# Three column blocks of the second modulation multiplied and added up on GpSimd in a hybrid S5 and attention block on one Trainium2 core

## Chip, core and metric

The kernel runs on one core of one Trainium2 chip. The metric is the device time of one execution in microseconds (us). Everything here is one launch; weights, input and output lie in the chip's memory outside the core.

## The reference, cut to what is computed

One decoder layer over 256 tokens of width 2048:

```python
mod = silu(c) @ w_ada + b_ada
shift1, scale1, gate1, shift2, scale2, gate2 = split(mod, 6)
h = rms(x, norm1_w) * (1 + scale1) + shift1
u, q, k, v = split(h @ w_in)
y_ssm = s5_mixer(u)
y_att = dilated_attention(q, k, v)
x = x + gate1 * (concat([y_ssm, y_att]) @ w_out)
h2 = rms(x, norm2_w) * (1 + scale2) + shift2
x = x + gate2 * ((silu(h2 @ w_ffn_gate) * (h2 @ w_ffn_up)) @ w_ffn_down)
```

`mod` is a product of one row, `silu(c)`, with a matrix of 2048 x 12288: nearly all of its cost is to read the matrix. The second modulation is `shift2` and `scale2`, each 2048 columns, cut into four blocks of 512 columns: eight blocks. They are needed only when `h2` is made, after the output projection.

## The kernel before

All big products run in pairs of rounded halves: ScalarE copies a loaded weight tile into `whi` (L135), VectorE makes the rest `wlo` (L137), and TensorE multiplies three times (`mm_tok`, L154). Each weight tile is 128 x 1024 floats, 512 KB. SyncE's queue issues all of them in an order fixed by the program (`load`, L110), into a **ring of six buffers** named `raw`. Load n+6 goes into the buffer of load n, so it is issued only when all who read load n are done, and every later load stands behind it in that queue.

The stages in order: the first modulation together with the products for `u` and the first `q` block; then five blocks of q, k and v columns, eight weight tiles each, so 40 steps of twelve matmuls over 512 columns (tile `qkv`); eight steps for the gate of the S5 part (tile `z`); 32 steps of the output projection (`wo`, `wol`); then the feed-forward part (`ff`, `dn`).

After each weight tile's matmuls, `step()` lets side work advance. Side work is made of Python generators: `lanes` (S5 batches `ssm_batch` with products S and y, attention heads `head`, query and key posts), and the modulation stream `ada_stream`, which is advanced 1.6 times per step in the first 30 steps and 0.9 times after. One advance of the stream stands for about one load of `w_ada`. A cost that a generator hands back is taken from the budget of 2.2 that the lanes get in a step.

In `ada_stream` a load of `w_ada` goes through TensorE: a column of `silu(c)` against the tile (L255, tile `ada`). A block of 512 columns is eight loads. After a set of blocks the sums are copied out and turned into columns by a small matmul, `ada_finish` (L212, tile `adac`). `DV` names blocks that do not go this way: `ada_dve` takes them, one block here (scale2's last). VectorE multiplies each half tile by a column of `silu(c)` and adds it to `gv` in one instruction (L310, L312), sixteen per block, and `ada_finish` turns `gv` with four matmuls against ones. `ada_next` would mix this generator in from its 80th call on; the stream drains it before that, at its own end (L271). After that the stream waits until seven of eight S5 batches are done and then goes through `gate1`, 32 loads on VectorE (L292).

GpSimd clears tiles (L512 to L589, L277) and issues the DMAs that reorder the S5 output: `yd` to memory (L780), then four `yT` back (L783), for each of eight batches.

Which instruction stands where on SyncE is the program's order. On the other engines a scheduler sets it when the program is built, from priorities in program order and its own estimate of when operands are ready. An engine runs its list in order and stops at a wait.

Of the kernel before, what the change touches and what calls it, by code (L numbers as in the profile page):

```python
# [11 lines left out]
ALU = mybir.AluOpType  # L12
# [26 lines left out]
NEX = 1.6  # L39
NEX2 = 0.9  # L40
NDB = 7
DV = ((4, 12, 4),)
DV0 = 80
DVS = 6
GPE = ()
QN_ACT = True
NS1 = 30
# [14 lines left out]
def body(tc, sm, tabs, bc, brow, x, wada, wg2, win, wglu, wout, wgate, wup, wdown, out):  # L62
    nc = tc.nc
    V, A, PE, G, SP = nc.vector, nc.scalar, nc.tensor, nc.gpsimd, nc.sync
# [43 lines left out]
    def load(src):  # L108
        raw = ring.tile([128, 2, 512], F32, name="raw", bufs=RAW)
        SP.dma_start(raw.rearrange("p k n -> p (k n)"), src)  # L110
        return raw
# [95 lines left out]
    def ada_finish(parts, ev, whole=False):  # L207
        kind, g0, ng = parts[0]
        n = len(parts)
        pc = ms([128, ng, n], "adac")  # L210
        for j in range(ng):
            PE.matmul(pc[:, j], lhsT=ev[:, j * 128:(j + 1) * 128], rhs=ones[:, 0:1] if whole else sel[:, 0:n], start=True, stop=True)  # L212
        for i, (kind, g0, _) in enumerate(parts):
            cols = slice(g0, g0 + ng)
            n, bn, wn = MOD[kind]
            V.tensor_tensor(out=gcol[n][:, cols], in0=pc[:, :, i], in1=col(bn)[:, cols], op=ALU.add)
            if wn:
                V.scalar_tensor_tensor(out=gcol[n][:, cols], in0=gcol[n][:, cols], scalar=1.0, in1=col(wn)[:, cols],
                                       op0=ALU.add, op1=ALU.mult)
        if kind < 2:  # L220
            h_hook[0](g0 // 2)

    def ada_stream(sets):
# [45 lines left out]
            yield  # L269
        ada_finish(*pend)  # L270
        for _ in adv:  # L271
            yield 1.2
        while len(done_b) < NDB:
            yield
        g = P8([128, D], "gate1")
# [5 lines left out]
        for b in range(4):  # L281
            gb = g[:, b * 512:(b + 1) * 512]
            ps = ada_ps
            for h in range(8):
                wt = load(wada[8 + b, h])
# [15 lines left out]
    def ada_dve():  # L301

        for kind, g0, ng in DV:
            gv = p1.tile([128, 512], F32, name="gv", tag="gv", bufs=1)
            for h in range(8):
                wt = load(wada[kind * 4 + g0 // 4, h])
                for j in range(2):
                    c = cs[:, 2 * h + j:2 * h + j + 1]
                    if h + j == 0:
                        ts(gv, wt[:, j], c, None, ALU.mult)  # L310
                    else:
                        V.scalar_tensor_tensor(out=gv, in0=wt[:, j], scalar=c, in1=gv, op0=ALU.mult, op1=ALU.add)  # L312
                yield 1.2
            yield
            ada_finish([(kind, g0, ng)], gv, True)

    ada = ada_stream([[(0, 2 * p, 2), (1, 2 * p, 2)] for p in range(8)]
                     + [[v for v in [(k, 4 * b, 4) for b in range(4)] if v not in DV] for k in (3, 4)])
    adv = ada_dve()
    adn = [0]  # L320

    def ada_next():
        adn[0] += 1
        if adn[0] >= DV0 and adn[0] % DVS == 0:
            c = next(adv, -1.0)
            if c != -1.0:
                return c or 0.0
        return next(ada, None) or 0.0


# [38 lines left out]
    def ts(o, a, s1_, s2_, o0, o1=None):  # L369
        if o1 is None:  # L370
            V.tensor_scalar(out=o, in0=a, scalar1=s1_, scalar2=None, op0=o0)
        else:
            V.tensor_scalar(out=o, in0=a, scalar1=s1_, scalar2=s2_, op0=o0, op1=o1)
# [511 lines left out]
    nstep = [0]  # L885

    def one(ln):

        while ln:
            try:  # L890
                return next(ln[0])
            except StopIteration:
                ln.pop(0)
        return None
# [6 lines left out]
    def step(budget=SB):  # L901
        nstep[0] += 1
        debt[0] = max(debt[0] - budget, -budget)
        pace = lambda n: int(min(n, NS1) * NEX + max(n - NS1, 0) * NEX2)
        for _ in range(pace(nstep[0]) - pace(nstep[0] - 1)):
            debt[0] += ada_next()
        turn[0] ^= 1
        live = [{0: turn[0], 1: 1 - turn[0], 2: 2, 3: 3}[i] for i in LORD] * LM
        stop = set()
        for k in live:  # L910
            if debt[0] < 0 and k not in stop:
                c_ = one(lanes[k])
                if c_ is None:
                    stop.add(k)
                else:
                    debt[0] += c_
# [8 lines left out]
    for b in range(2):  # L925
        for which, blk in ((0, 2 + b), (1, 4 + b), (2, 6 + b)):
            if blk == 2:
                lanes[3].append(qk_post(b, which, q0))
                continue
            ps = acc([128, 2, 512], "qkv")  # L930
            for hf in range(8):
                hl = take()
                for j in range(2):
                    kc = hf * 2 + j
                    mm_tok(ps, lambda a, t: hT[kc // 4][:, kc % 4, a, t * 128:(t + 1) * 128], hl, j, kc == 0, kc == 15)
                step()
            if which < 2:
                lanes[3].append(qk_post(b, which, ps))
            else:
                lanes[3].append(v_post(b, ps))  # L940
                for h in range(4):
                    lanes[2 + h % 2 * b].append(head(b, h))
# [3 lines left out]
    for nb in range(2):  # L946
        z = acc([128, 4, 256], "z")
        for hf in range(4):
            hl = take()
            for j in range(2):  # L950
                kc = hf * 2 + j
                for c in range(4):
                    w = slice(c * 128, c * 128 + 128)
                    for n, (wt, a) in enumerate(((hl[0], 0), (hl[0], 1), (hl[1], 0))):
                        PE.matmul(z[:, c], lhsT=wt[:, j, w], rhs=yT[kc // 4][:, kc % 4, a], start=(kc == 0 and n == 0 and c % 2 == 0),
                                  stop=(kc == 7 and n == 2), skip_group_check=True)
            step()
        th_ = T4([128, 4, 256], "zth")
        nat = lambda v: v.rearrange("p m (r j) -> p m j r", r=4)
        tq = lambda v: v.rearrange("p m (j r) -> p m j r", r=4)  # L960
        for c in range(4):
            A.activation(tq(th_)[:, c], nat(z)[:, c], AF.Tanh, scale=0.5)
        yy = T4([128, 4, 256], "zy")
        for c in range(4):
            tt(tq(yy)[:, c], nat(yT[nb][:, :, 0].bitcast(F32))[:, c], nat(yT[nb][:, :, 1].bitcast(F32))[:, c], ALU.add)
        V.scalar_tensor_tensor(out=yy, in0=th_, scalar=1.0, in1=yy, op0=ALU.add, op1=ALU.mult)
        mt = act.tile([128, 4, 2, 256], F32R, name="mixS", tag="act", bufs=4)
        A.mul(mt[:, :, 0], yy, 0.5)
        V.scalar_tensor_tensor(out=mt[:, :, 1], in0=yy, scalar=0.5, in1=mt[:, :, 0].bitcast(F32), op0=ALU.mult, op1=ALU.subtract)
        mix.append(mt)  # L970
# [307 lines left out]
```

## Time and profile before

| what | value |
|---|---|
| median of three runs | 1247.48 us (1246.68 to 1251.21) |
| the profiled execution, its own time | 1248.12 us |
| its span, first to last instruction | 1246.3 us |
| TensorE busy (matmul) in the span | 1193.3 us |
| VectorE busy | 793.3 us |
| GpSimd busy | 50.5 us |

The table's busy times are sums over the whole span; a stage has its own limit, so the rows below are taken by stretches. A busy TensorE is not TensorE at its peak: spacing between matmuls is read from the chain of waits. Waits are put down to whichever awaited event came last.

### The profile page before, as it was taken

The numbers are of one execution on the slowest core, as the hardware profiler recorded it, in microseconds if no ns is written. First come the engines' busy times: TensorE is split into PE (matmuls) and PEld (weight loads), VectorE is DVE, ScalarE is ACT, GpSimd is POOL, SyncE is SP. The second block draws the span as 40 slices with busy tenths as digits, with TensorE's granted clock in tenths as the row PEclk, the third lists the DMA queues.
The fourth block names the chain that finished last, engine by engine and source line by source line (L and its number), as shares of the span: only waits on it lengthen the run. The fifth ranks groups of instructions, "written<-read, shape, count | busy, mean of one in ns | idle before, by whom it ended". The sixth has DMA issues, their size and how long they took to land.

```text
span 1246.3 us, 17021 instructions
## 1 busy us (share of the span) xinstructions
PE 1193.3 (96%) x6312; PEld 954.0 (77%) x6312; DVE 793.3 (64%) x1402; ACT 572.2 (46%) x871; POOL 50.5 (4%) x90
## 2 busy tenths in 40 slices
PE   4789899999998999899999999999999999999998
PEld 2567667667797777688888888888888878888886
DVE  7964766477879998855665565565555444545544
ACT  3654574456455445644444444444444443434332
POOL 1110001121120000000000000000000000000000
PEclk9899999999999999899999999999999999999999
DMA  9889878897996899367777777777766656666662
GB/s 378 314 289 365 311 265 293 287 305 265 327 318 205 300 338 338 120 212 241 233 241 224 240 241 241 230 228 248 236 187 187 197 161 199 207 197 205 197 208 67
DMA packets 93906, 306.85 MB, mean 246 GB/s; under 512 B 18080, under 2 KB 20544, under 8 KB 93184
## 3 DMA queue, kind: packets, MB, share of 16 engines
q1 hardware_dynamic: 80784, 294.69, 70.7%
q0 software_dynamic: 11312, 6.70, 2.7%
q10 hardware_dynamic: 1728, 4.38, 0.9%
q8 instruction: 49, 0.80, 0.3%
q14 instruction: 33, 0.27, 0.1%
HBM read 301.54 MB, written 4.19 MB: 245 GB/s over the span
## 4 chain that ended last, share of the span: by engine, by line
PE 79%; DVE 10%; DMA 5%; ACT 3%; issue 2%; POOL 0%; DVEq 0%; ACTq 0%; POOLq 0%
PE ff L154 38%; PE dn L154 14%; PE qkv L154 8%; PE dnl L154 5%; PE ada L255 3%; DMA raw<-wada 3%; DVE wlo L137 2%; PE uacc L639 2%; PE wo L154 2%; DMA raw<-win 1%; PE y L763 1%; PE S L733 1%; DVE gate L292 1%; PE q L154 1%; DVE wkt L368 1%
## 5 line engine op out<-in xcount | busy, mean ns | idle before, releaser
L137 DVE TENSOR_TENSOR wlo<-raw,whi 128x1024 fp32r<-128x1024 f32 x365 | 446.6, 1224 | 334.5 <-ACT whi L135 333.8
L135 ACT CAST whi<-raw 128x1024 fp32r<-128x1024 f32 x365 | 384.8, 1056 | 499.3 <-PE ff L154 270.1
L154 PE MATMUL ff<-whi,h2T 128*128 128x512 f32 x1408 | 438.5, 391 | 0.7 <-DVE h2T L1074 0.5
L154 PEld LDWEIGHTS ff<-whi,h2T 128*128 128x128 f32 x1408 | 264.6, 188 | 56.6 <-ACT h2T L1073 1.0
L154 PE MATMUL ff<-wlo,h2T 128*128 128x512 f32 x704 | 274.5, 390 | 0.0
L154 PE MATMUL dn<-whi,aT 128*128 128x512 f32 x528 | 163.4, 390 | 0.0
L154 PEld LDWEIGHTS ff<-wlo,h2T 128*128 128x128 f32 x704 | 132.5, 188 | 26.9
L154 PEld LDWEIGHTS dn<-whi,aT 128*128 128x128 f32 x528 | 99.1, 188 | 21.0 <-ACT whi L135 0.2
L154 PE MATMUL qkv<-whi,hT 128*128 128x512 f32 x320 | 108.1, 405 | 0.3 <-ACT whi L135 0.2
L154 PE MATMUL dn<-wlo,aT 128*128 128x512 f32 x264 | 103.1, 391 | 0.0
L154 PEld LDWEIGHTS qkv<-whi,hT 128*128 128x128 f32 x320 | 60.6, 190 | 25.5 <-issue 6.4
L154 PE MATMUL qkv<-wlo,hT 128*128 128x512 f32 x160 | 64.1, 401 | 2.0 <-DVE wlo L137 2.0
L1132 DVE SCALAR_TENSOR_TENSOR gate<-raw,cs,gate 128x1024 f32<-128x1024 f32 x32 | 41.1, 1284 | 38.3 <-DMA raw<-wg 38.3
L639 PE MATMUL uacc<-hT,whi 128*128 128x256 f32 x256 | 51.7, 299 | 6.9 <-ACT whi L135 6.9
L154 PEld LDWEIGHTS dn<-wlo,aT 128*128 128x128 f32 x264 | 49.6, 188 | 10.8 <-issue 0.5
L154 PE MATMUL dnl<-whi,aT 128*128 128x512 f32 x176 | 54.4, 389 | 0.0
L292 DVE SCALAR_TENSOR_TENSOR gate<-raw,cs,gate 128x512 f32<-128x512 f32 x64 | 48.0, 754 | 7.6 <-DMA raw<-wada 7.2
L639 PEld LDWEIGHTS uacc<-hT,whi 128*128 128x128 f32 x256 | 42.0, 201 | 13.5 <-ACT whi L135 9.9
L255 PE MATMUL ada<-raw,c 128*4 128x256 f32 (+1 forms) x496 | 50.7, 492 | 0.0
L639 PE MATMUL uacc<-hT,wlo 128*128 128x256 f32 x128 | 38.7, 302 | 5.7 <-DVE wlo L137 5.7
L154 PEld LDWEIGHTS dnl<-whi,aT 128*128 128x128 f32 x176 | 33.0, 188 | 7.0 <-DVE o L368 0.2
L154 PEld LDWEIGHTS qkv<-wlo,hT 128*128 128x128 f32 x160 | 30.5, 191 | 8.9 <-DVE wlo L137 2.3
(318 smaller groups left out, 1257.1 us busy)
## 6 DMA issues: line engine op xcount, KB each, us to landing
raw<-wada SPq DMA_DIRECT2D x130, 512.0 KB, 5.3
raw<-wgate SPq DMA_DIRECT2D x88, 512.0 KB, 4.3
raw<-wup SPq DMA_DIRECT2D x88, 512.0 KB, 4.1
raw<-wdown SPq DMA_DIRECT2D x88, 512.0 KB, 3.7
raw<-win SPq DMA_DIRECT2D x64, 512.0 KB, 5.5
raw<-wout SPq DMA_DIRECT2D x32, 512.0 KB, 4.9
raw<-wg SPq DMA_DIRECT2D x32, 512.0 KB, 4.0
rawp<-wada SPq DMA_DIRECT2D x30, 512.0 KB, 7.2
```

The lines of the kernel that those rows point to most:

```text
L135: A.copy(hi, raw)
L137: V.tensor_tensor(out=lo, in0=raw, in1=hi.bitcast(F32), op=ALU.subtract)
L154: PE.matmul(ps[t] if type(ps) is list else ps[:, t], lhsT=lhs(a, t), rhs=w[:, j], start=first and n == 0, stop=last and n == 2)
L255: PE.matmul(ps[32 * q:32 * q + 4, 0:w], lhsT=c7[:, kc, 3 - i:7 - i], rhs=wts[t][:, j * w:(j + 1) * w], start=q not in seen, stop=n == len( ...
L292: V.scalar_tensor_tensor(out=gb, in0=wt[:, j], scalar=cs[:, 2 * h + j:2 * h + j + 1], in1=gb, op0=ALU.mult, op1=ALU.add)
L368: V.tensor_tensor(out=o, in0=a, in1=b, op=op)
L639: PE.matmul(uacc[b][:, c], lhsT=wt[:, j, w], rhs=h[:, j, a], start=(kc == 0 and n == 0 and c % 2 == 0), stop=(kc == 15 and n == 2), skip_g ...
L733: PE.matmul(S[:, e, Q], lhsT=wv[:, 0, Q, e].rearrange("p i c -> p (i c)"), rhs=U[:, m, Q], start=True, stop=True)
L763: PE.matmul(y[:, Q], lhsT=Vt[:, Q, e].rearrange("p r c -> p (r c)"), rhs=hp[:, e, Q], start=False, stop=e == 1, skip_group_check=True)
L1132: V.scalar_tensor_tensor(out=g, in0=wt, scalar=cs[:, k:k + 1], in1=g, op0=ALU.mult, op1=ALU.add)
```

## The change

`DV` now names three blocks of scale2: columns 512 to 1023, 1024 to 1535 and 1536 to 2047. The first two leave `ada_stream` and so TensorE; the third was VectorE's. `ada_dve` now puts all three on GpSimd. What was one instruction of VectorE per half tile is two of GpSimd: a multiplication by a column in place (`raw` into `raw`, after the first half tile) and an addition to `gv`. `gv` still has one buffer. The generator hands back no cost any more. `step()` advances it 0.7 times per step by itself, and `ada_stream` still drains what is left of it when its own blocks are done.

```diff
-DV = ((4, 12, 4),)
-DV0 = 80
-DVS = 6
+DV = ((4, 4, 4), (4, 8, 4), (4, 12, 4))
+NPL = 0.7
@@ ada_stream
         for _ in adv:
-            yield 1.2
+            yield
@@ ada_dve
                     if h + j == 0:
-                        ts(gv, wt[:, j], c, None, ALU.mult)
+                        G.tensor_scalar(out=gv, in0=wt[:, j], scalar1=c, scalar2=None, op0=ALU.mult)
                     else:
-                        V.scalar_tensor_tensor(out=gv, in0=wt[:, j], scalar=c, in1=gv, op0=ALU.mult, op1=ALU.add)
-                yield 1.2
+                        G.tensor_scalar(out=wt[:, j], in0=wt[:, j], scalar1=c, scalar2=None, op0=ALU.mult)
+                        G.tensor_tensor(out=gv, in0=wt[:, j], in1=gv, op=ALU.add)
+                yield
@@ ada_next
-        adn[0] += 1
-        if adn[0] >= DV0 and adn[0] % DVS == 0:
-            c = next(adv, -1.0)
-            if c != -1.0:
-                return c or 0.0
         return next(ada, None) or 0.0
@@ step
         for _ in range(pace(nstep[0]) - pace(nstep[0] - 1)):
             debt[0] += ada_next()
+        if int(nstep[0] * NPL) > int((nstep[0] - 1) * NPL):
+            next(adv, None)
```

The built programs show what moved, at three places. In the changed file line numbers are a little lower: L109 is the load, L153 the big matmul, L211 the matmul of `ada_finish`, L309 to L312 the GpSimd instructions, L775 and L778 the reordering DMAs.

SyncE's queue in the second half of the q, k, v steps, before (`win` is a weight tile of a step; `wada` is a load of the modulation, here two at a time for TensorE, and after the `x3` one at a time for VectorE's block):

```order
L110 DMA raw<-win 128x1024 x2
L110 DMA raw<-wada 128x1024 x2
L110 DMA raw<-win 128x1024
L110 DMA raw<-wada 128x1024 x2
L110 DMA raw<-win 128x1024
L110 DMA raw<-wada 128x1024 x2
L110 DMA raw<-win 128x1024
L110 DMA raw<-wada 128x1024 x2
L110 DMA raw<-win 128x1024 x3
L110 DMA raw<-wada 128x1024
L110 DMA raw<-win 128x1024
```

The same queue in the change, from the same place; the first row is in both programs the 163rd and 164th load, counted from zero over all loads of that queue:

```order
L109 DMA raw<-win 128x1024 x2
L109 DMA raw<-wada 128x1024 x3
L109 DMA raw<-win 128x1024
L109 DMA raw<-wada 128x1024
L109 DMA raw<-win 128x1024
L109 DMA raw<-wada 128x1024 x2
L109 DMA raw<-win 128x1024
L109 DMA raw<-wada 128x1024 x3
L109 DMA raw<-win 128x1024
L109 DMA raw<-wada 128x1024 x2
L109 DMA raw<-win 128x1024 x13
L109 DMA raw<-wada 128x1024
```

All eleven `wada` loads ahead of the `x13` are GpSimd's now, with four `win` between them; TensorE's own loads of the modulation have all passed. The last `wada` is `gate1`'s first.

GpSimd's list in the change, near the end of its third block (`gv` is the running sum; the brackets name the counters that an instruction waits on, `Pool_49` being GpSimd's own):

```order
L311 TENSOR_SCALAR raw<-raw,cs 128x512
L312 TENSOR_TENSOR gv<-raw,gv 128x512 [waits Pool_49]
L775 DMA yd<-wks 256x1x256 [waits DMASW5_49,DVE_49]
L312 TENSOR_TENSOR gv<-raw,gv 128x512 [waits Pool_49]
L311 TENSOR_SCALAR raw<-raw,cs 128x512 [waits DMAHW4_49]
L311 TENSOR_SCALAR raw<-raw,cs 128x512
L312 TENSOR_TENSOR gv<-raw,gv 128x512 [waits Pool_49]
L778 DMA yT_1982<-yd 32x8x64 [waits DMASW6_49,DMASW5_49]
L312 TENSOR_TENSOR gv<-raw,gv 128x512 [waits Pool_49]
L311 TENSOR_SCALAR raw<-raw,cs 128x512 [waits DMAHW7_49,DMAHW5_49]
```

Four instructions now stand there per load, each addition waits for GpSimd's own earlier work, and the reordering DMAs stand in between.

TensorE's list in the change, at the end of the second `gv` block (`adac` is the small matmul on `gv`; `qkv` of the next weight tile stands behind it):

```order
L153 MATMUL qkv<-wlo,hT 128x512
L153 MATMUL qkv<-whi,hT 128x512
L211 MATMUL adac<-ones,gv 128x1 [waits PE_49,Pool_49]
L211 MATMUL adac<-ones,gv 128x1 x3
L728 MATMUL S<-U,wv 128x64 [waits PE_49]
```

Such a wait of TensorE on GpSimd stands at three places now, one per block. The third stands right behind the twelve matmuls of the first of the thirteen `win` tiles. Before, the one `adac` on `gv` waited for VectorE and stood among the `z` matmuls.

## Rows read from the trace of the kernel before

**Rows 1.** Busy time by stretch: length, busy us (instructions) per engine, clock, DMA share, GB/s

```profile
171.00:230.00 59.00, 56.65 (x325) 40.64 (x326) 43.38 (x122) 31.77 (x91) 7.85 (x16) 0.97 0.84 281
230.00:290.00 60.00, 57.27 (x358) 39.31 (x356) 37.51 (x106) 29.45 (x58) 9.84 (x15) 1.00 0.89 279
290.00:355.00 65.00, 65.00 (x384) 50.71 (x384) 54.23 (x129) 34.38 (x86) 9.02 (x13) 1.00 0.93 311
355.00:402.00 47.00, 43.94 (x298) 39.97 (x298) 40.32 (x82) 27.67 (x51) 6.31 (x11) 1.00 0.82 246
402.00:450.00 48.00, 46.77 (x207) 36.18 (x206) 44.45 (x78) 24.28 (x38) 0.57 (x1) 1.00 0.90 310
450.00:512.00 62.00, 58.13 (x257) 46.83 (x255) 53.36 (x92) 30.65 (x53) 0.00 (x0) 0.94 0.78 278
```

**Rows 2.** Waits of SyncE's queue from 171 to 316 us: total, times, longest

```profile
SPq L110 <- PE ada L255: 68.5, 21, 7.1
SPq L110 <- DVE wlo L137: 17.5, 8, 3.6
```

**Rows 3.** SyncE's issues in order of time: start, length, what, count

```profile
174.27 0.33 SPq L110 DMA_DIRECT2D raw<-win  x1
...
289.34 0.38 SPq L110 DMA_DIRECT2D raw<-win  x1
```

**Rows 4.** The chain that ended last, 262 to 356 us: start, length, what, count

```profile
313.97 2.95 PE qkv L154 x12
316.92 0.97 PE ada L255 x8
...
335.47 0.79 PE adac L212 x8
...
343.31 5.50 PE qkv L154 x24
```

**Rows 5.** TensorE in order of time: the first matmul of z

```profile
363.50 0.59 PE L955 MATMUL z<-yT,whi 128*128 128x256 f32 x2
```

**Rows 6.** Groups of GpSimd: count, busy us, mean ns, idle before and its releaser

```profile
L783 POOL DMA_DIRECT2D yT<-yd x32 | 19.3, 671 | 21.1 <-DMA yd<-wks 21.1
L546 POOL MEMSET wst<- 128x1024 f32 x8 | 7.7, 971 | 74.1 <-PE pk L583 41.2 <-DVE bct L368 26.3 <-PE qtp L820 6.6
...
L780 POOL DMA_DIRECT2D yd<-wks x8 | 5.7, 721 | 75.4 <-DVE wks L777 75.4
...
L277 POOL MEMSET gate<- 128x2048 f32 x1 | 1.8, 1805 | 33.9 <-PE y L763 33.9
```

**Rows 7.** Groups of all engines, same columns: modulation on TensorE and VectorE, and `wlo`

```profile
L137 DVE TENSOR_TENSOR wlo<-raw,whi 128x1024 fp32r<-128x1024 f32 x365 | 446.6, 1224 | 334.5 <-ACT whi L135 333.8 <-issue 0.2
...
L255 PE MATMUL ada<-raw,c 128*4 128x512 f32 x224 | 31.3, 592 | 0.0
...
L312 DVE SCALAR_TENSOR_TENSOR gv<-raw,cs,gv 128x512 f32<-128x512 f32 x15 | 11.2, 748 | 0.2
```

**Rows 8.** DMA issues on the page: operation, count, KB each, us to landing

```profile
raw<-wada SPq DMA_DIRECT2D x130, 512.0 KB, 5.3
```

**Rows 9.** Waits of TensorE from 355 to 512 us: total, times, longest

```profile
PE rsb L1064 <- DVE dg L373: 3.9, 1, 3.9
PE z L955 <- DVE wlo L137: 2.9, 2, 2.5
```

## The prediction, made before the changed kernel ran

> **What bounds the kernel now.** I read the profile by stretches first [rows 1]. From 171 us, where the q, k, v steps begin, to 512 us, where the feed-forward part is under way, TensorE shows 93 to 100% busy and VectorE 63 to 93%, with the DMAs at 0.78 to 0.93. The change lies wholly in there; after it TensorE runs without gaps to the end. So every microsecond by which the feed-forward part starts later or earlier is one on the result.
>
> Next, what holds back the loads. From 171 to 316 us SyncE waits longest for TensorE to be done with `ada` loads, 68.5 us in 21 waits, and 17.5 us for `wlo` [rows 2]. The reader should see in this that the ring of six is what couples the engines: a load that anyone holds long holds up all loads behind it, those of `qkv` too. From the load at place 105 to that at 163 the queue needs 289.34 - 174.27 = 115.1 us for 58 loads [rows 3].
>
> Then the pace of TensorE itself from the chain of waits [rows 4]: 24 `qkv` matmuls in 5.50 us, so 2.75 us for a weight tile; eight `ada` instructions, which are two loads, in 0.97 us, so 0.485 us for a load; an `adac` group 0.79 us. The twelve matmuls that end at 316.92 us are those of the 52nd of 64 `win` tiles; twelve tiles come after. The first `z` matmul starts at 363.50 us [rows 5], so twelve tiles (33 us) and 13.6 us of other matmuls lie between.
>
> **The change, part by part.**
>
> *Off TensorE.* Two blocks are 16 loads x 0.485 = 7.8 us. Two more groups of `adac` come in, 2 x 0.79 = 1.6 us. Net 6.2 us less work. The trace has 224 instructions for seven blocks, 32 each, which agrees with four per load [rows 7].
>
> *Off VectorE.* Sixteen instructions of 748 ns [rows 7], 12.0 us. VectorE is not what TensorE waits for most of the time, so this pays only where it is: in `z`, 2.9 us, and ahead of the second norm, 3.9 us [rows 9]; all of TensorE's missing busy time from 355 to 512 us is 8.2 us [rows 1]. Bounds 0 and 8.2. I take 4, because the wait ahead of the norm is a chain of small instructions that this does not shorten.
>
> *Onto GpSimd.* Per load two multiplications and two additions of 512 elements. The trace has GpSimd only clearing and issuing DMAs [rows 6]. Clearing 2048 elements takes 1805 ns and 1024 take 971, so 0.814 ns an element and 0.14 us fixed; 512 would be 0.55 us. If reading hides behind writing, all four cost that: 2.2 us a load. If each operand passes one after the other, a multiplication moves 1024 elements (0.97 us) and an addition 1536 (1.39 us): 4.7 us. Nothing suggests a price below clearing. I take **4.2 us**, near the upper end, since in the third excerpt each addition waits for GpSimd's own work before it, so that nothing overlaps from one to the next. The library instruction ahead of the first multiplication stands once, early, where GpSimd has slack: bounds 0 and 1.8 us, the longest instruction there now, taken as nothing.
>
> The Trainium skill (GPSIMD Engine Reference, section on performance versus the Vector engine) speaks against such a move: it calls GpSimd the wrong choice for ordinary elementwise work and gives 4497 ns for an addition of 2048 floats. An estimate from that page is 1.1 us an addition, with one-input work near line rate, so about 3.4 us a load. By it the sum below would be 9 us lower.
>
> *Where GpSimd's time falls.* The pace of 0.7 per step does not hold: when `ada_stream` has no blocks left it drains the rest, and the second excerpt shows eleven GpSimd loads with four `win` among them, behind place 164. TensorE cannot run past them in two ways. Load n+6 waits for GpSimd; and TensorE stops at `adac` at the end of the second block, and again behind the first of the thirteen `win` tiles, with everything else queued behind it. So the end of the third block sets when the last twelve tiles start.
>
> 1. Place 163 in the queue comes at 289.3 us before. Between 105 and it stand 36 `ada` loads and 21 `win` tiles before, 28 and 17 now with 12 loads of GpSimd: TensorE has 8 x 0.485 + 4 x 2.75 = 14.9 us less to do. The bound from below is 0; from above, the DMAs at 311/0.93 = 334 GB/s need 1.57 us for 512 KB, 91 us for 58 loads, 24 us less than 115.1. I take 12, near the TensorE figure and a little less because GpSimd's waits for `yd` now hold ring buffers too. 277.3 us.
> 2. Place 165 is issued two loads later (3 us) and lands 5.3 us after [rows 8]: 285.6 us.
> 3. Eleven loads x 4.2 = 46.2 us: 331.8 us.
> 4. In between, on the same engine, one `yd` (0.72), three `yT` (2.0) and the wait for `yd` to land (21.1/8 = 2.6 on average) [rows 6]: 337.1 us.
> 5. One `adac`, 0.8 us: 337.9 us, against 316.9 before. **21.0 us later.**
>
> TensorE has 7 tiles and some 4 us of S and y to do meanwhile, 23 us; it idles the rest.
>
> *After that.* Twelve tiles are left in both. Beside them I count in the change three y groups, one S, two `qtp`, two heads' scores: some 14 us against 13.6, the same. About one head's work (2 us) is then done before `z` and not after. With VectorE's 4 us: 21.0 - 2 - 4 = **15 us**. `gate1` starts earlier in the queue and ends earlier; that is in the 4. The `yT` DMAs that now stand behind additions are read only by `z`, which itself starts later; nothing if that cover holds, and a few us if `z` is not delayed.
>
> Against its own time the profiled execution gives 1248.1 + 15 = 1263.1 us. It lies 0.6 us above the median of the runs, so I forecast **1262 us**.
>
> **The rivals.**
>
> *GpSimd keeps up (faster).* If a load costs 2.2 us as clearing does, step 3 shrinks by 22 us and the third block ends at 315.9, when TensorE has come about as far as before. If in addition place 163 comes 19 us sooner rather than 12, it ends at 308.9, no wait is left, and the removed work pays: 6.2 + 4 = 10 us less, 1237 us. It decides at 2.8 us a load with my other terms (the point of no change is 15/11 below 4.2), at 3.5 with place 163 at its earlier time. For it: SyncE's 68.5 us of waits were for TensorE, and now twelve of those loads ahead of place 163 are held by an engine that is idle 84% there. Against it: two operands and an own wait per addition.
>
> *It balances out.* Near 2.8 us a load, or 3.5 with the early ring: 1247 us.
>
> *GpSimd and VectorE get in each other's way.* If an instruction of one that reads two tiles keeps the other's from starting, each GpSimd instruction would wait on average half a `wlo` (0.61 us) for the 70% of the time that VectorE is busy: 0.43 x 4 = 1.7 us more a load, 19 us more in step 3, so 1281 us, and `wlo` late as well. The Trainium skill (SBUF — State Buffer, section on who interferes with whom) has such a rule: a VectorE instruction with two inputs in SBUF and a GpSimd instruction that reads SBUF exclude each other for a whole instruction. No row here shows it, since GpSimd reads nothing in the kernel before.
>
> That GpSimd does not do this work at all is ruled out by the third excerpt.
>
> **How the numbers follow.** A measurement of this kernel tells 0.5%, 6.2 us, from no change. Forecast 0.48; contention 0.17; balance 0.19, which lies within 0.5%; keeping up 0.16. So faster 0.16, same 0.19, slower 0.65. The range runs from 1241, which leaves out the rival of keeping up, to 1285, just past contention. The likeliest case alone spans 1254 to 1280: at the upper end 4.7 us a load (+5.5) and place 163 at its old time (+12); at the lower the middle of the two bounds, 3.45 us a load (-8.3).
>
> **What would show it.** In the profile after: a GpSimd group of multiplications at 0.5 to 1.0 us and additions at 1.1 to 1.4; SyncE's longest waits in this stretch on GpSimd's `gv`; TensorE idle some 20 us between 280 and 340 us, put down to GpSimd at `adac` or to late `whi`; the first `z` matmul near 384 us instead of 363.5; and the distance from there to the end 4 to 8 us shorter. It is wrong if additions come at 0.6 us, if `z` starts before 368 us, or if the loss lies after `z`.

## The result and the profile after

| what | before | after |
|---|---|---|
| median | 1247.38 us (4 runs, 1246.68 to 1251.21) | 1335.01 us (4 runs, 1330.13 to 1335.09) |
| ratio | | 1.068, interval 1.065 to 1.071: slower |
| the profiled execution, and its span | 1248.12, 1246.3 us | 1335.05, 1332.9 us |
| GpSimd busy / VectorE busy | 50.5 / 793.3 us | 201.8 / 821.4 us |

The loss is 87.6 us; 15 were forecast. VectorE lost 11.7 us of work (its sixteen `gv` instructions) and is busy 28.1 us longer, so its other instructions take 39.8 us more. Summed by groups, some 10 us of this growth are in instructions of eight columns, 9 in the scans of 64 columns, 13 in instructions of 252 to 512 columns on S5 tiles, and 2 in `wlo`. Two of the groups, which had means of 272 and 168 ns in the kernel before (x64 and x4):

```profile
L743 DVE TENSOR_TENSOR_SCAN wks<-ss_rho,wks 128x64 f32<-128x64 f32 x64 | 21.7, 400 | 0.0
L97 DVE TENSOR_SCALAR rsyq<-rsyq 128x8 int32<-128x8 int32 x4 | 6.3, 1568 | 0.1
```

The windows of the kernel after answer to [rows 1] (length, busy us and instructions of PE, PEld, DVE, ACT, POOL, granted clock, DMA share, GB/s):

```profile
171.00:230.00 59.00, 47.88 (x271) 33.88 (x269) 41.01 (x85) 26.24 (x80) 35.40 (x33) 0.96 0.76 247
230.00:290.00 60.00, 43.00 (x209) 29.22 (x210) 37.61 (x82) 15.80 (x30) 39.30 (x34) 0.81 0.68 208
290.00:325.00 35.00, 27.89 (x168) 18.08 (x165) 26.70 (x62) 18.92 (x38) 24.44 (x15) 0.94 0.76 265
325.00:400.00 75.00, 35.72 (x134) 29.66 (x134) 28.90 (x48) 14.36 (x37) 72.41 (x49) 0.66 0.43 138
400.00:458.00 58.00, 58.00 (x308) 50.83 (x308) 41.40 (x96) 28.20 (x64) 12.75 (x19) 0.92 0.69 191
458.00:512.00 54.00, 52.68 (x335) 46.64 (x334) 53.22 (x103) 31.95 (x57) 0.00 (x0) 1.00 0.78 272
```

From the start of the q, k, v steps TensorE is 72 to 81% busy where it was 95% and more, so the loss does not begin at the eleven loads but with the first block. From 325 to 400 us GpSimd alone sets the pace, 72.41 of 75 us; the DMAs carry 138 GB/s.

The waits of SyncE's queue from 165 to 480 us (total, times, longest); [rows 2] are of 171 to 316 us, and over 165 to 480 us the kernel before has 76.8 for `wlo`, 79.2 for `ada` and 5.2 for `gv`:

```profile
SPq L109 <- DVE wlo L136: 81.6, 26, 8.9
SPq L109 <- POOL gv L312: 74.3, 17, 7.3
SPq L109 <- PE ada L254: 67.8, 18, 6.2
```

SyncE's issues in order of time, places 163 to 167 [rows 3]; the row x2 is places 163 and 164:

```profile
316.07 0.86 SPq L109 DMA_DIRECT2D raw<-win  x2
318.25 5.03 SPq L109 DMA_DIRECT2D raw<-wada  x3
```

GpSimd's groups (busy us, mean ns, idle before and its releaser), new beside [rows 6]:

```profile
L311 POOL TENSOR_SCALAR raw<-raw,cs 128x512 f32<-128x512 f32 x45 | 82.5, 1843 | 27.1 <-DMA raw<-wada 23.4 <-DVE rstq L99 3.0 <-issue 0.6
L312 POOL TENSOR_TENSOR gv<-raw,gv 128x512 f32<-128x512 f32 x45 | 65.0, 1444 | 1.1
```

A load costs 2 x 1.843 + 2 x 1.444 = 6.6 us on average. GpSimd's own order of time shows two multiplications that were held up (the row x2, beside a `wlo` of VectorE's), and a multiplication and an addition that were not:

```profile
325.16 5.20 POOL L311 TENSOR_SCALAR raw<-raw,cs 128x512 f32<-128x512 f32 x2
...
337.25 1.56 POOL L311 TENSOR_SCALAR raw<-raw,cs 128x512 f32<-128x512 f32 x1
338.78 1.26 POOL L312 TENSOR_TENSOR gv<-raw,gv 128x512 f32<-128x512 f32 x1
```

Undisturbed that is 2 x (1.56 + 1.26) = 5.6 us a load.

The chain of waits around the end of the third block, to be held against [rows 4]:

```profile
393.19 3.09 POOL raw L311 x2
396.29 1.23 POOL gv L312
...
398.10 1.28 POOL gv L312
...
399.43 1.87 PE adac L211 x8
...
407.16 4.07 PE qkv L153 x12
```

and, in TensorE's order of time, the first `z` matmul, to be held against [rows 5]:

```profile
457.66 0.41 PE L952 MATMUL z<-yT,whi 128*128 128x256 f32 x2
```

The `adac` group starts when GpSimd's last addition ends. It stands ahead of all thirteen `win` tiles: 156 of the 480 `qkv` matmuls start after it. The section on the change, and with it the prediction, has the first of the thirteen in front of it. Twelve `qkv` matmuls then take 4.07 us where they took 2.95. TensorE's granted clock was 0.66 in the 75 us up to 400, a mean between its two levels (1.2 and 2.4 GHz), and TensorE had been busy less than half of that time; the clock rose as follows (same columns as above):

```profile
399.43:407.16 7.73, 7.73 (x36) 7.73 (x37) 1.47 (x3) 1.29 (x2) 1.08 (x2) 0.50 0.92 287
407.16:411.23 4.07, 4.07 (x14) 3.21 (x14) 1.15 (x3) 1.21 (x3) 0.00 (x0) 0.67 0.01 4
411.23:414.75 3.52, 3.52 (x34) 3.52 (x33) 2.40 (x4) 1.95 (x3) 0.55 (x1) 1.00 0.11 12
```

TensorE's waits from 165 to 480 us:

```profile
PE adac L211 <- POOL gv L312: 25.0, 3, 14.7
PE qkv L153 <- DVE wlo L136: 18.9, 8, 6.1
PE qkv L153 <- ACT qn L803: 13.2, 1, 13.2
```

and ScalarE's in the same time, which say what `qn`, the normed queries and keys, was waiting for (10.3 us in all, 3.7 the longest, in the kernel before):

```profile
ACT qn L803 <- DVE rsyq L102: 23.5, 4, 12.0
```

`rsyq` is a chain of VectorE instructions of eight columns each. Ahead of TensorE's wait of 13.2 us, which ended at 373.67, its first and last instruction were

```profile
364.44 1.06 DVE L368 TENSOR_SCALAR ssq<-ssq 128x8 f32<-128x8 f32 x1
...
370.22 1.19 DVE L102 TENSOR_TENSOR rsyq<-rsyq,rstq 128x8 f32<-128x8 f32 x1
```

so it took 7.0 us; undisturbed, fourteen of its fifteen instructions take 2.8 us (377.64 to 380.44 in the run e4 below). Some 4 of the 13.2 us are thus VectorE's growth. The rest is not: the next matmul in TensorE's list needed `qn`, and nothing else stood in front of it.

The difference of the spans, 86.6 us, divides by these rows: the third block's `adac` ends 401.3 - 316.9 = 84.4 us after the mark of step 5; from there to `z` 56.4 us instead of 46.6, 9.8 more; from `z` to the end 875.2 instead of 882.8, 7.6 less.

Last, VectorE's order of time between 233 and 239 us:

```profile
233.76 4.81 DVE L97 TENSOR_SCALAR rsyq<-rsyq 128x8 int32<-128x8 int32 x1
234.92 3.65 DVE L743 TENSOR_TENSOR_SCAN wks<-ss_rho,wks 128x64 f32<-128x64 f32 x1
```

and GpSimd's beside it:

```profile
230.49 4.68 POOL L311 TENSOR_SCALAR raw<-raw,cs 128x512 f32<-128x512 f32 x2
235.14 1.27 POOL L312 TENSOR_TENSOR gv<-raw,gv 128x512 f32<-128x512 f32 x1
236.37 0.94 POOL L541 MEMSET wst<- 128x1024 f32 x1
237.28 1.26 POOL L312 TENSOR_TENSOR gv<-raw,gv 128x512 f32<-128x512 f32 x1
```

An instruction of 8 columns, 168 ns in the kernel before, stands for 4.81 us and ends at 238.57, when GpSimd's back-to-back run ends (238.54); the scan stands behind it. What is behind that is tested below.

### The profile page after: what moved, and what is told of

It reads as the page before. It is cut to its first block, busy times and chain, and to the rows that moved or that the text cites. A ratio compares the mean times of both kernels' runs of the same rounds, so it can differ in the third digit from the quotient of the medians.

```text
span 1332.9 us, 17036 instructions
## 1 busy us (share of the span) xinstructions
PE 1215.4 (91%) x6264; PEld 975.2 (73%) x6264; DVE 821.4 (62%) x1386; ACT 569.6 (43%) x871; POOL 201.8 (15%) x183
## 4 chain that ended last, share of the span: by engine, by line
PE 62%; DVE 4%; POOL 4%; DMA 2%; issue 2%; ACT 0%; DVEq 0%; ACTq 0%; POOLq 0%; SPq 0%
PE ff L153 36%; PE dn L153 13%; PE dnl L153 4%; PE qkv L153 3%; POOL raw L311 2%; POOL gv L312 2%; DMA raw<-wout 1%; DVE wlo L136 1%; PE wol L153 1%; PE z L952 1%; DVE gate L291 1%; PE atp L1151 1%; DMA raw<-wada 1%; PE y L758 1%; DVE xg L363 0%
## 5 line engine op out<-in xcount | busy, mean ns | idle before, releaser
L136 DVE TENSOR_TENSOR wlo<-raw,whi 128x1024 fp32r<-128x1024 f32 x365 | 448.4, 1230 | 350.2 <-ACT whi L134 348.9
L153 PE MATMUL ff<-whi,h2T 128*128 128x512 f32 x1408 | 437.3, 390 | 1.5 <-ACT h2T L1070 0.9
L153 PEld LDWEIGHTS ff<-whi,h2T 128*128 128x128 f32 x1408 | 264.1, 188 | 57.8 <-ACT h2T L1070 1.8
L153 PE MATMUL ff<-wlo,h2T 128*128 128x512 f32 x704 | 274.0, 389 | 0.0
L153 PE MATMUL dn<-whi,aT 128*128 128x512 f32 x528 | 163.4, 390 | 0.0
L153 PEld LDWEIGHTS ff<-wlo,h2T 128*128 128x128 f32 x704 | 132.2, 188 | 27.1
L153 PE MATMUL qkv<-whi,hT 128*128 128x512 f32 x320 | 119.2, 443 | 21.7 <-ACT qn L803 13.2
L153 PEld LDWEIGHTS dn<-whi,aT 128*128 128x128 f32 x528 | 99.1, 188 | 21.0 <-ACT whi L134 0.2
L153 PE MATMUL dn<-wlo,aT 128*128 128x512 f32 x264 | 103.1, 391 | 0.0
L153 PEld LDWEIGHTS qkv<-whi,hT 128*128 128x128 f32 x320 | 68.7, 215 | 43.6 <-ACT whi L134 13.4
L153 PE MATMUL qkv<-wlo,hT 128*128 128x512 f32 x160 | 71.8, 449 | 18.9 <-DVE wlo L136 18.9
L311 POOL TENSOR_SCALAR raw<-raw,cs 128x512 f32<-128x512 f32 x45 | 82.5, 1843 | 27.1 <-DMA raw<-wada 23.4
L1129 DVE SCALAR_TENSOR_TENSOR gate<-raw,cs,gate 128x1024 f32<-128x1024 f32 x32 | 41.1, 1285 | 45.9 <-DMA raw<-wg 45.9
L312 POOL TENSOR_TENSOR gv<-raw,gv 128x512 f32<-128x512 f32 x45 | 65.0, 1444 | 1.1
L153 PEld LDWEIGHTS dn<-wlo,aT 128*128 128x128 f32 x264 | 49.6, 188 | 10.7 <-issue 0.5
L153 PEld LDWEIGHTS qkv<-wlo,hT 128*128 128x128 f32 x160 | 34.7, 217 | 29.5 <-DVE wlo L136 22.6
L153 PE MATMUL dnl<-whi,aT 128*128 128x512 f32 x176 | 54.4, 390 | 0.0
L634 PEld LDWEIGHTS uacc<-hT,whi 128*128 128x128 f32 x256 | 44.4, 212 | 13.2 <-ACT whi L134 9.9
```

Source lines behind the costliest of these rows:

```text
L136: V.tensor_tensor(out=lo, in0=raw, in1=hi.bitcast(F32), op=ALU.subtract)
L153: PE.matmul(ps[t] if type(ps) is list else ps[:, t], lhsT=lhs(a, t), rhs=w[:, j], start=first and n == 0, stop=last and n == 2)
L311: G.tensor_scalar(out=wt[:, j], in0=wt[:, j], scalar1=c, scalar2=None, op0=ALU.mult)
L312: G.tensor_tensor(out=gv, in0=wt[:, j], in1=gv, op=ALU.add)
L634: PE.matmul(uacc[b][:, c], lhsT=wt[:, j, w], rhs=h[:, j, a], start=(kc == 0 and n == 0 and c % 2 == 0), stop=(kc == 15 and n == 2), skip_g ...
L1129: V.scalar_tensor_tensor(out=g, in0=wt, scalar=cs[:, k:k + 1], in1=g, op0=ALU.mult, op1=ALU.add)
```

## The experiments

Three theories. **A, hold**: GpSimd keeps a ring buffer for 6.6 us a load, SyncE's queue stands behind it, and TensorE stands at `adac`. **B, keep out**: GpSimd and VectorE delay each other, so `wlo` and small VectorE work come late. **C, places**: the loads stand badly in the queue, 2.3 a step early and thirteen `win` alone later. All runs here are single, profiled ones; each is held against the kernel before on the same chip (1248.15 to 1251.24 us). A single run tells some 6 us from nothing. Edits are against the changed kernel where nothing else is said, and cut to the lines that carry them.

**e1: VectorE at the same places.**

```diff
-G.tensor_scalar(out=wt[:, j], ...); G.tensor_tensor(out=gv, ...)
+V.scalar_tensor_tensor(out=gv, in0=wt[:, j], scalar=c, in1=gv, op0=ALU.mult, op1=ALU.add)
```

> The three blocks are loaded at the same places of the queue as in the change, but VectorE multiplies and adds them in one instruction per half tile, as the kernel before did with its one block. Theory A (GpSimd's own time per load, 6.6 us, held in the ring of six): no such hold is left, the time falls to 1240 to 1262 us (VectorE has 24 us more work than before, TensorE 6 us less). Theory B (GpSimd and VectorE keep each other from starting): the same 1240 to 1262 us. Rival C (the places in the queue, eleven loads of a kind with four weight tiles among them, are what costs): 1300 us or more.

Measured 1275.53, 24.3 over the kernel before, between the two expectations. So 63 of 88 us belong to GpSimd, and 24 to the places and to VectorE's 24 us of additional work, which this run does not divide.

**e2: one block on GpSimd**, the other two through TensorE: `DV = ((4, 12, 4),)`.

> Only the block that VectorE had before goes to GpSimd, eight loads at the pace of 0.7 per step; the other two go through TensorE as before. The drain then finds nothing left, so the loads stand singly. Theory A: eight holds of 6.6 us against steps of 4.4 us, 4.6 us of GpSimd time per step, a loss of 5 to 15 us: 1250 to 1262 us. Theory B: a third of GpSimd's instructions, a third of the loss of 87.6: about 1276 us. Rival C: no cluster, no loss: 1240 to 1250 us.

Measured 1274.65, +23.4: one block loses more than a quarter of what three lose, although SyncE waits only 9.8 us for `gv`.

**e17: the same one block at the same places on VectorE** (e2 with e1's edit).

> The kernel with one block on GpSimd, its block on VectorE instead, at the same places (early, 0.7 a step beside the stream). The kernel with one block on GpSimd lost 27 us. Theory C (places): this one loses the same, 1268 to 1278 us. Theories A and B (it is GpSimd): 1245 to 1255 us.

Measured 1257.68, +6.9, between the two expectations. One block moved from VectorE to GpSimd costs 16.5 us at these places; the places cost some 7, hardly more than a single run can tell.

**e11: the kernel before, its one block on GpSimd at the old places.**

> The kernel before, with its one VectorE block on GpSimd at the same places of the queue (two instructions for one, 8 loads). Nothing else moves. Theory A (hold): eight loads, each with one win behind it, cost GpSimd 8 x 6.6 = 53 us where the kernel before takes 8 x (2.75 TensorE) = 22 to 30 us for the same stretch, so some 20 to 30 us later, 1267 to 1278 us. Theory B: the same sign, and less here, since it lasts 50 us only: 1255 to 1267 us. Theory C (places): no change, 1243 to 1251 us.

Measured 1269.92, +19.1, as A said and 3 us above B's range; C's "no change" falls. SyncE's waits in that stretch have a new row:

```profile
SPq L110 <- POOL gv L313: 39.9, 7, 8.0
```

**e3: additions only** (the multiplication in place is left out) and **e4: clears instead** (the blocks' arithmetic is left out; GpSimd clears each load six times):

```diff
-G.tensor_scalar(out=wt[:, j], ...); G.tensor_tensor(out=gv, ...)
+for _ in range(6): G.memset(wt, 0.0)      # e4, per load
```

> As the change, but the multiplications in place are left out (all but the first half tile of a block), so scale2's three blocks are plain sums of rows. GpSimd's time per load falls from 6.6 to about 2.7 us, 83 us less in all. Theory A: the last eleven loads take 35 us and not 74, and by the sum of the prediction, whose point of no change was 2.8 us a load, the time is 1240 to 1260 us. Theory B: the additions read two tiles and still exclude VectorE, 44% of the GpSimd time with reads is left, so 35 to 40 us of the loss: 1280 to 1290 us. Rival C: 1310 us or more.

> As the change, but GpSimd clears the loaded tile six times (6 x 0.96 us) in place of multiplying and adding, so scale2's three blocks come out without their product. It holds each load for 5.8 us, about what its four instructions need when nothing disturbs them (2 x 1.56 + 2 x 1.26 = 5.6 us), but reads nothing. Theory A: the hold alone sets the time, 1305 to 1325 us. Theory B: VectorE's long instructions vanish (a TENSOR_SCALAR of 8 columns that took up to 4.8 us, a scan up to 3.7 us) and with them most of the loss of the first part: 1265 to 1295 us.

e3 took 1301.99, +50.8, in none of the three ranges: 44% of the change's GpSimd work (66.8 of 151.3 us) leaves 58% of its loss. e4 took 1339.52, +88.3, above both ranges and as much as the change itself, though a clear reads nothing. VectorE's group of four small instructions (0.7 us in the kernel before) shows why e4 does not divide A from B:

```profile
L370 DVE TENSOR_SCALAR ssq<-ssq 128x8 f32<-128x8 f32 x4 | 32.1, 8028 | 0.1
```

One of the four, in VectorE's order of time:

```profile
346.29 31.31 DVE L370 TENSOR_SCALAR ssq<-ssq 128x8 f32<-128x8 f32 x1
377.64 0.17 DVE L96 TENSOR_SCALAR rsyq<-ssq 128x8 int32<-128x8 int32 x1
```

and GpSimd's at that time:

```profile
344.47 33.10 POOL L313 MEMSET raw<- 128x1024 f32 x37
```

A VectorE instruction of 0.165 us stood for 31.31 us, until 37 clears in a row had ended (377.57). It did not get in between two of them.

**e6: no wait of TensorE.** `ada_finish` of the three blocks is left out.

```diff
-            ada_finish([(kind, g0, ng)], gv, True)
+            V.memset(gcol['g2'][:, g0:g0 + ng], 1.0)
```

> The three GpSimd blocks are multiplied and added as in the changed kernel, but their sums are not turned into columns: the twelve adac matmuls that read gv are left out and the columns of scale2 that they make are set to a constant, so TensorE never waits for GpSimd. The loads, their places and GpSimd's work stay. Theory A (hold): what costs time is the buffer that GpSimd keeps for 6.6 us a load, and the queue behind it; the 25.0 us that TensorE waits at adac would otherwise be waited for late weight tiles. Expected 1318 to 1335 us, with TensorE's waits moving to whi and wlo. Theory A' (the product at the end of a block): the 25.0 us are lost only because TensorE's order puts adac there; expected 1305 to 1312 us. By both the first z matmul stays as far from the end as in the changed kernel, 875 us.

Measured 1313.85, +65.7: 21.9 us less than the change, between the two and near A' (which had 25). The place of `adac` in TensorE's order is a loss of its own; three quarters of the whole remain without it.

**e12: side work alone**, GpSimd's 96 instructions on a tile that nobody else reads.

> All eight blocks go through TensorE. GpSimd does the same number of instructions of the same kind and size as in the changed kernel (48 multiplications by a column, 48 additions), but on a tile of its own that no one else reads and that is no buffer of the ring; a few steps each, from the start of q, k, v on. So no load is held and no one waits for GpSimd, save its own DMAs of the S5 output. Theory A (hold): within 1244 to 1258 us. Theory B (GpSimd and VectorE keep each other out): VectorE's sum grows by some 25 to 40 us as in the changed kernel, and TensorE waits for wlo and for qn, 1265 to 1310 us. A single number for B: half of the 60 us that stand between the changed kernel and e1, 1280 us.

Measured 1333.01, +84.9, above every range, but it doesn't answer the question. The work waits for nothing of the stage that it was meant for, and the scheduler put it early: it lies between 9.5 and 165.9 us. These are windows of this run; in the kernel before TensorE was busy 70.1 us in the first:

```profile
40.00:120.00 80.00, 40.06 (x308) 29.50 (x308) 54.03 (x126) 19.64 (x53) 76.17 (x54) 0.66 0.39 143
120.00:171.00 51.00, 14.87 (x102) 12.66 (x103) 17.83 (x34) 14.80 (x31) 44.36 (x35) 0.61 0.26 85
```

There GpSimd's clears for the S5 tables (`te`, L589) stand in its list among the side work. ScalarE waits for them, and TensorE for ScalarE's `whi`, from 40 to 171 us:

```profile
ACT te L600 <- POOL te L589: 51.2, 3, 19.7
PE uacc L639 <- ACT whi L135: 36.6, 3, 20.5
```

In the kernel before these two waits are 1.2 and 5.2 us. The three long ones of ScalarE run from 85.9 to 104.1, 112.3 to 125.6 and 143.5 to 163.2 us, and TensorE stands idle from 91.0 to 105.3, 119.8 to 133.4 and 145.0 to 165.6. So what e12 lost early is in the main the wait for GpSimd's own clears, and not B.

**e16: side work tied to its place**; all blocks through TensorE, each second q, k, v step:

```diff
+V.tensor_copy(c, w[:, 0, 0:1].bitcast(F32))          # one column of wlo
+for _ in range(2):
+    G.tensor_scalar(out=gv, in0=gv, scalar1=c, scalar2=None, op0=ALU.mult)
+    G.tensor_tensor(out=gv, in0=gv, in1=gv, op=ALU.add)
```

**e10: its base, the kernel before with all blocks through TensorE** (`DV = ()`).

> As the kernel with side work alone, but the work is tied to its place: in each second of the 40 q, k, v steps VectorE copies one column of wlo, and GpSimd's two multiplications (by that column) and two additions on a tile of its own, 128x480, wait for it: 80 instructions, some 110 us of GpSimd's time between 175 and 330 us. All blocks go through TensorE, no load is held, and TensorE, ScalarE and VectorE wait for nothing of this work; only GpSimd's own DMAs of the S5 output stand behind it. Theory B (GpSimd and VectorE keep each other out): small VectorE instructions grow to some us as in the changed kernel, TensorE waits for wlo and qn, and the first z comes 25 to 60 us later than in the kernel before, 1275 to 1310 us. Theory A (hold): the first z within 8 us of 363.5, 1244 to 1256 us.

> The kernel before with all eight blocks through TensorE: the base of the pinned side work, which has the same loads. One more block on TensorE is 8 x 0.485 = 3.9 us, less 0.8 for an adac group, and VectorE is 12 us freer. Expected 1244 to 1253 us; so the side work's 1273.9 would be 21 to 30 us from GpSimd alone. If it came out near 1260 us, half of that loss would be TensorE's.

e16 took 1273.94, +23.1; e10 1252.37, +2.5. So **20.7 us come from GpSimd's work alone**, with no load held and nobody waiting for a result; B is shown, at a price below its lowest forecast. Not all of it need be keeping out: GpSimd's own clears and DMAs stand behind the side work here too, and from 165 to 480 us ScalarE's longest wait for a clear of `te` is 7.5 us (0.3 in e10) and its longest for a `yd` to land 10.1 (5.6 in e10). How the 20.7 divide between the two is not shown. VectorE is busy 815.7 us against e10's 783.6; less 3.0 for the twenty copies its instructions grew by 29.1 us. GpSimd's multiplications in e16, as a group:

```profile
L913 POOL TENSOR_SCALAR gv<-gv,tiny 128x480 f32<-128x480 f32 x40 | 80.1, 2003 | 46.6 <-DVE tiny L911 36.4 <-DVE rstq L100 5.1 <-DVE rstq L101 2.8
```

and two of VectorE's groups, which had means of 272 and 161 ns in the kernel before:

```profile
L748 DVE TENSOR_TENSOR_SCAN wks<-ss_rho,wks 128x64 f32<-128x64 f32 x64 | 18.5, 351 | 0.0
L100 DVE TENSOR_TENSOR rstq<-rsyq 128x8 f32<-128x8 f32 x12 | 4.6, 380 | 0.2
```

**e20: the hold alone.** The loads stand as in the change and GpSimd's queue holds them, by chained small DMAs; the three blocks' sums are left out.

```diff
-G.tensor_scalar(out=wt[:, j], ...); G.tensor_tensor(out=gv, ...)
+G.dma_start(scr, wt[:, j, 0:64])          # scr: one tile in memory, so each waits for the last
```

> The loads of the three blocks stand where the changed kernel has them and are held by GpSimd's queue, but GpSimd computes nothing: for each half tile it issues a small DMA of 128x64 from the load to memory, and the second waits until the first has landed, as does the next load's. So the three blocks' sums are left out (gv is cleared and turned into columns as before). How long a load is then held is read from the run; some 5 to 9 us by the landing times of the S5 output's small DMAs. Theory A (hold), if the hold is near 6.6 us: what is left of the changed kernel's 88 us without the 23 us of the pinned side work, 1300 to 1325 us. Theory B (GpSimd and VectorE keep each other out is most of it): 1260 to 1280 us, VectorE's sum down by the 11.7 us that it no longer does.

Measured 1292.87, +43.0, between the two. The hold came out as wanted: GpSimd's order of time has the first DMAs of three loads in a row at

```profile
341.08 0.58 POOL L313 DMA_DIRECT2D scr<-raw  x1 [0.25 <-DMA scr<-raw]
...
347.43 0.58 POOL L313 DMA_DIRECT2D scr<-raw  x1 [0.85 <-DMA scr<-raw]
...
354.46 0.54 POOL L313 DMA_DIRECT2D scr<-raw  x1 [1.46 <-DMA scr<-raw]
```

(354.46 - 341.08) / 2 = 6.7 us a load; over all 24 loads the mean from the first DMA's issue to the second's landing is 7.9 us, so the hold is rather longer than the change's. The longest in total of SyncE's waits from 165 to 480 us is then

```profile
SPq L109 <- DMA scr<-raw: 75.7, 22, 6.9
```

which is the change's 74.3 us for `gv` again, and VectorE is undisturbed: 785.2 us against 793.3 - 11.7 = 781.6. Since `gv` is only cleared here, TensorE does not stand at `adac`.

**e13, e14, e18, e21, e22: the loads mixed** into the stream, each second turn (e14 and e22 on VectorE). The stream keeps its old pace in e13, e14 and e18, where it comes so late that the output projection reads some of `gate1` before it is complete; in e21 and e22 it is advanced 0.95 times a step, instead of 0.9, after the 30th, and nothing is left out:

```diff
+        adn[0] += 1
+        if adn[0] >= DV0 and adn[0] % 2 == 0:      # DV0: 1 in e13, e14; 8 after
+            c = next(adv, -1.0)
```

> Three blocks on GpSimd as in the changed kernel, but the loads stand elsewhere in the queue: each second turn of the modulation stream goes to them from the first q, k, v step on, so that the loads of w_ada come at the old pace (1.6 a step, then 0.9) and none are drained together. Theory C (places: 2.3 loads a step early, eleven together, then thirteen win alone) says that some 27 us of the loss go: 1300 to 1312 us. Theory A (hold): GpSimd needs 24 loads x 6.6 us = 158 us wherever they stand, 171 + 158 = 329 us at best against 399 in the changed kernel, and the rest of TensorE's work fits beside it: 1265 to 1285 us. Theory B: VectorE stays hindered, 1285 to 1300 us.

> The same places as in the mixed kernel, the three blocks on VectorE (one instruction for each half tile), nothing on GpSimd. With e1 it shows what places cost without GpSimd. Theory C: e1's 25 us over the kernel before go, 1240 to 1253 us. Rival: VectorE's 24 us of additional work in this stretch, not the places, is what e1 lost; then 1265 to 1280 us as in e1.

> The mixed kernel again with three blocks on GpSimd, the mixing begun at the eighth turn of the stream and not at the second, so that the first modulation is complete before the q, k, v products read it, as in the kernels before and after. The earlier one took 1320 us. Expected 1312 to 1330 us. If it comes near 1300 us or below, places were worth more than the earlier one said.

> The mixed kernel once more, with the stream 0.95 times a step after the 30th step instead of 0.9: in the two earlier mixed GpSimd kernels, and in the mixed VectorE one, the stream came so late that the output projection read some of gate1 before it was complete (amount and kinds of work were the same). Expected as the earlier ones, 1305 to 1325 us, by theories A and B; theory C (places) is refuted as the main cause if it is above 1300 us.

> The mixed VectorE kernel with the same mended pace. Expected 1255 to 1270 us (the earlier one took 1267). The distance to the mixed GpSimd kernel is what GpSimd costs in VectorE's place at equal places: 45 to 60 us by theories A and B, as between e1 and the changed kernel.

| run | blocks on | time (us) | over before (us) | first `z` matmul (us) |
|---|---|---|---|---|
| e13 | GpSimd | 1320.00 | 71.9 | 432.3 |
| e18 | GpSimd | 1307.44 | 56.6 | 417.8 |
| e21 | GpSimd | 1303.98 | 54.1 | 415.8 |
| e14 | VectorE | 1267.03 | 18.9 | 378.1 |
| e22 | VectorE | 1259.01 | 9.1 | 376.4 |

e13 came out above all three of its ranges, e14 where its rival had put it, e18 5 us and e21 1 us below theirs, and e22 within its own. The comparison rests on e21 and e22. At equal, better places GpSimd costs 54.1 - 9.1 = 45 us more than VectorE. Places are worth 15.2 us with three blocks on VectorE (e1 against e22) and 33.5 with GpSimd (the change against e21): a hold may hurt more where many held loads follow each other, which no run tests by itself. C is part of the loss, not its main cause. Nothing here beats the kernel before.

**The sum.** Hold and places without arithmetic (e20) 43.0; keeping out alone (e16 less e10) 20.7; the stop at `adac` (the change less e6) 21.9: 85.6 of the 87.6 us. The first two alone, 63.7, should be e6, which lost 65.7. That the parts simply add is an assumption, and this one agreement is all that supports it: e20 holds longer than the change, and e16 has 80 instructions where the change has 93. How e20's 43.0 divide between hold and places stays open. The places' share is 7 (e17, one block) to 15 us (e1 less e22), if it adds up; since e1 has e20's places and more VectorE work besides, and lost 24.3, at least some 18.7 should be the hold. Buffers of their own for GpSimd's loads, which would leave the arithmetic and take the hold away, were not tried.

## Why the prediction was wrong

The sign and the stage were right; the loss was forecast at 15 us and is 86.6 in the spans. The 71.6 us between them lie, by the prediction's own steps, in step 1 (38.8), step 2 (0.8), steps 3 and 4 (22.7), step 5 (1.1), the stretch from `adac` to `z` (9.8) and what lies behind `z` (-1.6).

- **Step 1 had the wrong sign**, the largest error: place 163 was said to come 12 us sooner (277.3) and came at 316.07, 26.7 later than in the kernel before. It was priced by TensorE's work alone, as if the twelve early loads were held by an idle engine and nothing else slowed; the price of a load was counted for the last eleven only. The place in three experiments, in SyncE's order of time (e20, e16, e10):

```profile
295.59 2.17 SPq L109 DMA_DIRECT2D raw<-win  x2
305.27 5.14 SPq L110 DMA_DIRECT2D raw<-win  x2
291.71 3.23 SPq L110 DMA_DIRECT2D raw<-win  x2
```

With the hold and no arithmetic it comes 6.3 us later than in the kernel before (e20), with GpSimd's arithmetic and no hold 13.6 later than its base (e16 less e10), and with the same places on VectorE 0.9 later (e1, 290.28). Leaving out TensorE's stop at `adac` changes little (e6, 314.85). So the hold alone is the smaller part of the 26.7, GpSimd's work beside VectorE's the larger, and some 7 are not divided.

- **The price of a load** (4.2 us, bounds 2.2 and 4.7) was outside its bounds: 5.6 us undisturbed, 6.6 on average. The addition came as forecast (1.26 us in 1.1 to 1.4). The multiplication did not: 1.56 us where 0.5 to 1.0 was said. The upper bound took one read and one write of 512 at a clear's pace per element; an operation that reads has its own price, which no row of clears bounds. The Trainium skill (GPSIMD Engine Reference, sections on performance versus the Vector engine and on engine selection), from which 3.4 us was estimated, erred the same way in that term: the multiplication, a one-input operation, which it places near line rate, is slower here than the addition.
- **Steps 3 and 4**: the last eleven loads took from 325.16 to 399.38, 74.2 us, step 4's own DMAs included, where the two steps had 51.5. Of the 22.7 more, 11 x (5.6 - 4.2) = 15.4 are the undisturbed price and 8.2 GpSimd's instructions grown beside VectorE's; GpSimd also idled 2.6 us, 2.1 of them before the third block's first instruction, and the DMAs took 2.0 us where 5.3 were counted.
- **The rival "get in each other's way" was the right mechanism, on the wrong side.** Its 1.7 us a load on GpSimd measured 6.6 - 5.6 = 1.0. The bulk is on VectorE: 39.8 us more, which the rival had only as "`wlo` late as well". `wlo` itself hardly grew (1230 ns against 1224 [rows 7]); smaller instructions did. The rival also took instructions that read two tiles; the longest stretches are of instructions with one input.
- **After that**: from `adac` to `z` no change was expected (14 us beside the twelve tiles against 13.6), and 9.8 us more came. One tile more stands there (2.75 us, thirteen and not twelve), the lower clock after the idle stretch costs some 4.3 by an estimate from the granted clock (0.50 to 407.16, then 0.67 to 411.23), and the rest is other work of TensorE's. None of this was a term of the sum. The 4 us on VectorE and 2 of head work behind `z` came together as 7.6; that their division was right isn't shown.
- TensorE's stop at `adac` was named in its place and put at about 20 us between 280 and 340; it was 25.0 us in three waits, and e6 gives it a price of 21.9 (single runs, so some 6 either way).

That the loss was likelier than not (0.65) was borne out; the range, 1241 to 1285, rested on bounds for the price of a load and for place 163, and both lay outside.

## What to carry to other kernels

A consumer that is slower per load than the engine it replaces is not "idle time used": in a ring with one queue in order, it holds every load behind it, so price the hold for all its loads, from the first, and not only where the engine is last. An engine new to a stage needs a row of its own kind of instruction before it is priced. And ask what its work does to the engine beside it, held loads or not, above all to small, chained instructions: their sum can grow where the largest ones' hardly does.

## What the runs showed of the hardware

- A one-input VectorE instruction on eight columns can be kept out by GpSimd's back-to-back run for as long as it lasts: 4.81 us beside arithmetic and a clear, 31.31 us beside 37 clears. The Trainium skill (SBUF — State Buffer, section on who interferes with whom) gives exclusion for a whole instruction, and names `tensor_scalar` among VectorE's operations that can take the shared ports; the traces agree that `TENSOR_SCALAR` is kept out, by clears too, but the wait outlasted many instructions of GpSimd.
- In the other direction GpSimd is kept out: in the change a multiplication takes 1.56 us with VectorE busy for less than 0.1 us of it (19 of 48), 2.33 where it overlaps a `wlo`, which has two inputs, by 0.2 us or more (16), and 1.85 on average. In e16, on 480 columns, it takes 2.00 on average.
- On GpSimd 512 floats in place cost more with one tile and a column (1.56 us) than with two tiles (1.26 us). A block's first multiplication, which isn't in place, took 1.57 at 174.22 us.
